# A two-layer decoder trunk on one core: 21 instead of 19 look-ahead groups, a new spacing of them, and the next chunk's weights split ahead of the second set of u dots

## The chip, the cores and the metric

The kernel runs on one core of one Trainium2 chip. The metric is the device time of one execution in microseconds (us). A profiled execution gives, beside its own time, a span (first to last instruction) and a trace of every engine: PE (matmuls), DVE (elementwise), ACT (activations, casts), POOL (here it issues gathers and scattered adds), SP (here it issues loads and stores).

## The reference

512 positions of width 1024 go through two layers. Each layer is a token mixer (layer 0: causal pooling beside retention; layer 1: a gated linear recurrence), an output projection, a residual and a layer norm, and then a PEER channel mixer with a residual and a layer norm. The change lies in PEER alone:

```python
q = (xt @ w_q).reshape(T, 8, 2, 128)
s = einsum('thpd,hpkd->thpk', q, sub_keys)
s_top, i_top = top_k(s, 16)
cand = s_top[:, :, 0, :, None] + s_top[:, :, 1, None, :]       # 256 per head
cand_id = i_top[:, :, 0, :, None] * 128 + i_top[:, :, 1, None, :]
best, pos = top_k(cand, 16)
eid = take_along_axis(cand_id, pos)                            # of 16384 experts
gate = softmax(best)
act = gelu(einsum('td,thkd->thk', xt, u_tab[eid]))
out = einsum('thk,thkd->td', gate * act, v_tab[eid])
```

## The kernel before

**How PEER is split.** The positions are four blocks of 128 (tb 0 to 3). Of 384 positions (tb 0 to 2) the sum over experts is made densely: 128 blocks of 128 experts, gathered into 32 groups of four. Per block, `mm1` (24 matmuls of 128x352, lines 185 to 187) makes x·u for 352 positions, ACT applies gelu into a tile `ge`, the result is multiplied with a dense gate tile `gt` (line 1059), and `mm2` (line 1096; 18 matmuls of 128x512: three position blocks, three products, two halves) multiplies with v. The last 128 positions, and the first 32 in another way, take gathered rows: `gather_rounds` fetches one u row and one v row per position and chosen expert (line 968), DVE makes a dot (line 980) and a weighted sum (line 993); for the 32 positions the u dots alone are gathered (`Scatter`, lines 102 to 105, gathers at line 741), and POOL adds their weights to a table `gz` (line 127).

**Hi and lo.** A product of float32 matrices is three passes: each weight block of 128x1024 is loaded by SP into one of five `raw` buffers, cast by ACT to `hi` (line 169), and DVE subtracts to make `lo` (line 170); the pairs have six buffers. Of each three matmuls, lines 185 and 186 use `hi` and line 187 uses `lo`.

**The stages of a layer.** Mixer and output projection; then `route_topk`, four chunks c of two heads each; then "choose" of tb 3, 1 and 2 (the second top-k, the softmax and `lookup`, all on DVE, and three transposes on PE, line 834); then `route_gates`, eight slices of two half-slices, each of which makes one-hot tiles `oh` and `og` on DVE (lines 900, 901), 32 small matmuls on PE (lines 910, 911), and a store of the slice's gates to `gd` in memory (line 916); then `experts`, which reads `gd` and `gz` back into `gt`. A chunk of `route_topk` begins with a projection of all 512 positions by four weight blocks w0 to w3 of `wq` (`proj_T`, 96 matmuls of 128x512, also on lines 185 to 187). If `self.w0` holds blocks that were split earlier, `wchunk` takes those; before the change, `route_topk` never sets it. Behind the projection follow, for each tb, the score matmuls and the top-k on DVE, and after tb 2 and tb 3 four u dots each.

**Work made ahead.** So that PE has work beside the routing, `lookahead` is a generator of `mm1` blocks: NLA groups of four. `peer` steps it by a credit: the two routing generators yield costs, and each 2.8 of credit takes one block. Blocks left when both generators have ended are made behind the last gate slice. The finished `ge` of a group is stored to memory (`sp`), except the last KEEP = 2 groups, and read back in `experts`. In `experts` such a group ("old") needs no `mm1` of its own and a "fresh" one does; fresh and old groups are interleaved, `mm1` runs four blocks ahead, and the gather rounds are paced with one unit per old block and two per fresh block.

**What sets the order.** The program text and the credit give the order in which work is handed to a list scheduler, which fixes the order of the instructions on each engine before the run. At run time each engine takes its instructions strictly in that order and waits, where it must, for buffers and semaphores.

Of the kernel before, what the change touches and what calls it, by code (L numbers as in the profile page):

```python
# [37 lines left out]
GQ = 8  # L38
LAG = GQ + 4
NSD = TD // 32  # L40
NLA = 19
NSZ = 4
KEEP = 2
ROT = 3
RAW = 5
QS = 8
Y2 = 1.85
YC = (1.5, 3.0, 3.0, 4.0)
AHEAD = 4
TAIL = 4  # L50
# [92 lines left out]
class Kern:  # L143
# [612 lines left out]
    def lookahead(self, layer, xT, sp):  # L756
        for g in range(NLA):
            ge = self.pe.tile([P, NB, TN], F32, name="ge", tag="ge", bufs=3)
# [8 lines left out]
    def route_topk(self, layer, xT, kT, gz):  # L767
        nc, tc, io = self.nc, self.tc, self.io
        with tc.tile_pool(name="rt", bufs=1) as rt, tc.tile_pool(name="rt2", bufs=2) as rt2, \
                tc.tile_pool(name="rs2", bufs=1) as rs2:  # L770
            i16 = rt.tile([P, 16], F16, name="i16", tag="i16")
            nc.gpsimd.iota(i16, pattern=[[1, 16]], base=0, channel_multiplier=0, allow_small_or_imprecise_dtypes=True)
            thr = rt.tile([P, 16], F16, name="thr", tag="thr")
            nc.sync.dma_start(out=thr, in_=io["thr"])
            stop = rt.tile([P, NTB, 16, 16], F32, name="stop", tag="stop")
            itop = rt.tile([P, NTB, 16, 16], F16, name="itop", tag="itop")
            wq = io["peer_w_q"][layer]

            def sink_q(n, ps):
                q = rt2.tile([P, T], F32, name="qh", tag="qh", bufs=5)  # L780
                nc.scalar.copy(q, ps)
                qs.append(q)

            def choose(tb, h0, n):
                sv = stop[:, tb, h0 * 2:(h0 + n) * 2].rearrange("p (h two) s -> p h two s", two=2)
                s0, s1 = sv[:, :, 0, :], sv[:, :, 1, :]
                iv = itop[:, tb, h0 * 2:(h0 + n) * 2].rearrange("p (h two) s -> p h two s", two=2)
                i0, i1 = iv[:, :, 0, :], iv[:, :, 1, :]
                cand = rs2.tile([P, 8, 64], F32, name="cand", tag="cand")
                at = 0  # L790
                for a, b, m in ((0, 1, 16), (1, 4, 8), (4, 8, 4), (8, 16, 1)):
                    w = b - a
                    ov = cand[:, :n, at:at + w * m].rearrange("p h (i j) -> p h i j", j=m)
                    nc.vector.tensor_tensor(ov, s0[:, :, a:b, None].broadcast_to([P, n, w, m]),
                                            s1[:, :, None, 0:m].broadcast_to([P, n, w, m]), ALU.add)
                    at += w * m
                best = rs2.tile([P, 8, 16], F32, name="best", tag="best")[:, :n]
                pos = rs2.tile([P, 8, 16], U32, name="pos", tag="pos")[:, :n]
                for h in range(n):
                    c2 = rs2.tile([P, 64], F32, name="c2", tag="c2")  # L800
                    cv = cand[:, h, :]
                    nc.vector.max(out=best[:, h, 0:8], in_=cv)
                    nc.vector.max_index(out=pos[:, h, 0:8], in_max=best[:, h, 0:8], in_values=cv)
                    nc.vector.match_replace(out=c2, in_to_replace=best[:, h, 0:8], in_values=cv, imm_value=NEG)
                    nc.vector.max(out=best[:, h, 8:16], in_=c2)
                    nc.vector.max_index(out=pos[:, h, 8:16], in_max=best[:, h, 8:16], in_values=c2)
                    yield 0.7
                if tb == 3:
                    gate = self.gate3.rearrange("p (h s) -> p h s", h=8)
                elif tb == 0:  # L810
                    gate = gz.gate[h0 // 2]
                else:
                    gate = rs2.tile([P, 8, 16], F32, name="gate", tag="gate")
                nc.vector.tensor_tensor(gate, best, best[:, :, 0:1].broadcast_to([P, n, 16]), ALU.subtract)
                nc.scalar.activation(gate, gate, AF.Exp)
                sm = rs2.tile([P, 8], F32, name="gsm", tag="gsm")[:, :n]
                nc.vector.tensor_reduce(sm, gate, AX.X, ALU.add)
                nc.vector.reciprocal(sm, sm)
                nc.vector.tensor_tensor(gate, gate, sm[:, :, None].broadcast_to([P, n, 16]), ALU.mult)
                kk = yield from self.lookup(rs2, pos, i0, i1, thr, i16)  # L820
                fl = "p h s -> p (h s)"
                if tb == 3:
                    nc.vector.scalar_tensor_tensor(self.eid, kk[0].rearrange(fl), 128.0, kk[1].rearrange(fl),
                                                   ALU.mult, ALU.add)
                    return
                if tb == 0:
                    gz.place(self, rs2, h0 // 2, kk[0].rearrange(fl), kk[1].rearrange(fl))
                    return
                tg = slice((tb - 1) * P // GW, tb * P // GW)
                ghT, glT = kT[:, tg, 2, :], kT[:, tg, 3, :]  # L830
                yield 2.8
                pt = self.psC.tile([P, 512], F32, name="pC", tag="pC")
                for i, t in enumerate((kk[0], kk[1], gate)):
                    nc.tensor.transpose(pt[:, i * P:(i + 1) * P], t.rearrange(fl), self.ident)
                px = pt[:, :3 * P].rearrange("p (i g w) -> p i g w", i=3, w=GW)
                nc.scalar.copy(kT[:, tg, 0:2, :].rearrange("p g i w -> p i g w"), px[:, 0:2])
                gs = rs2.tile([P, P // GW, GW], F32, name="gs", tag="gs")
                nc.scalar.mul(gs, px[:, 2], GS)
                nc.scalar.copy(ghT, gs)
                nc.vector.tensor_tensor(glT, gs, ghT, ALU.subtract)  # L840

            for c in range(4):
                qs = []
                keys = rt2.tile([P, 4, P], F32, name="keys", tag="keys")
                nc.sync.dma_start(out=keys, in_=io["keysT"][layer][:, c * 4:c * 4 + 4, :])
                self.proj_T(wq, c, xT, sink_q, early=c == 0)
                for tb in range(NTB):
                    ts = slice(tb * P, (tb + 1) * P)
                    ps = self.psB.tile([P, 512], F32, name="pB", tag="pB")
                    for i in range(4):  # L850
                        nc.tensor.matmul(ps[:, i * P:(i + 1) * P], qs[i][:, ts], keys[:, i, :],  # L851
                                         start=True, stop=True)
                    ixs = rs2.tile([P, 4, 16], U32, name="ix", tag="ix", bufs=2)
                    for i in range(4):
                        hp = c * 4 + i
                        sc = ps[:, i * P:(i + 1) * P]
                        mx = stop[:, tb, hp, :]
                        ix = ixs[:, i, :]
                        s2 = rs2.tile([P, P], F32, name="s2", tag="s2")
                        nc.vector.max(out=mx[:, 0:8], in_=sc)  # L860
                        nc.vector.max_index(out=ix[:, 0:8], in_max=mx[:, 0:8], in_values=sc)
                        nc.vector.match_replace(out=s2, in_to_replace=mx[:, 0:8], in_values=sc, imm_value=NEG)
                        nc.vector.max(out=mx[:, 8:16], in_=s2)
                        top = nc.vector.max_index(out=ix[:, 8:16], in_max=mx[:, 8:16], in_values=s2)
                    nc.vector.tensor_copy(itop[:, tb, c * 4:c * 4 + 4, :], ixs)
                    yield YC[c]
                    if tb == 0:
                        yield from choose(0, c * 2, 2)
                        if c:
                            gz.add(self)  # L870
                    else:
                        n = (0, 1, 1)[tb - 1] * QC // 2
                        yield 1.3 * n
                        with tc.issue_after(top.ins):
                            gz.dots(self, n)
                gz.weigh(self, rs2)
                if c == 0:
                    gz.add(self)
            gz.add(self, 8)
            for tb in (3, 1, 2):  # L880
                yield from choose(tb, 0, 8)
# [347 lines left out]
```

## Time and profile before

| | us |
|---|---|
| median of 3 runs | 2803.01 |
| lowest, highest | 2802.81, 2809.61 |
| profiled execution, its own time | 2803.68 |
| its span | 2801.9 |
| PE busy | 2745.8 (98%) |
| DVE busy | 2359.3 (84%) |

The profiled execution is 0.67 us above the median and 1.8 us above its span. Its mean granted PE clock is 0.992. Layer 0's PEER lies at about 200 to 1350 us of the span (choose about 440 to 505, gates to 613, experts from there), layer 1's at about 1660 to the end. In the wait views, a row is the waiting engine, tile and line, what it waited for, and then the total in us, the times and the longest. In the window views a row is the stretch, its length, then busy time and instruction count of PE, PEld (weight loads), DVE, ACT and POOL, the granted PE clock, the DMA engines' busy share, and GB/s. In timelines and chains a row begins with the start and the duration in us.

### The profile page before, as it was taken

How to read it: one execution, taken by the hardware profiler on the slowest of the kernel's cores; microseconds unless marked ns; L12 is line 12 of the kernel's file. 1: busy time of each engine (PE TensorE's matmuls, PEld its weight loads, DVE VectorE, ACT ScalarE, POOL GpSimd, SP SyncE). 2: the span in 40 equal slices, each digit the busy share in tenths (PEclk: the TensorE clock that was granted, in tenths of full speed). 3: DMA queues.
4: the chain of work that ended last, by engine and by line, in shares of the span. 5: the costliest groups of instructions: out<-in, count | busy, mean ns of one | idle time of the engine just before them, and what ended most of it. 6: DMA issues, size and time to landing. Idle time of an engine off the chain costs nothing.

```text
span 2801.9 us, 41670 instructions
## 1 busy us (share of the span) xinstructions
PE 2745.8 (98%) x15314; PEld 2449.4 (87%) x15314; DVE 2359.3 (84%) x4556; ACT 1116.5 (40%) x1575; POOL 1352.6 (48%) x865
## 2 busy tenths in 40 slices
PE   9999999999999999999999999999989999999998
PEld 7899899988888888888788898999978888888886
DVE  6678989867898989888798677899868888988887
ACT  3353336543333333333334343445543333333332
POOL 0006667864565666553000017667764556555651
PEclk9999999999999999999999999999999999999999
DMA  6357776999999999998222557686999999999993
GB/s 228 127 178 227 236 221 178 248 270 366 382 386 382 390 377 396 374 383 295 95 83 72 203 177 203 194 245 177 277 308 361 378 398 368 389 388 382 384 383 146
DMA packets 318318, 788.34 MB, mean 281 GB/s; under 512 B 62113, under 2 KB 128161, under 8 KB 318113
## 3 DMA queue, kind: packets, MB, share of 16 engines
q1 hardware_dynamic: 175808, 410.75, 41.4%
q0 software_dynamic: 120128, 303.22, 32.0%
q10 hardware_dynamic: 22176, 71.71, 6.4%
q8 instruction: 120, 1.97, 0.3%
q14 instruction: 86, 0.70, 0.1%
HBM read 708.50 MB, written 77.07 MB: 280 GB/s over the span
## 4 chain that ended last, share of the span: by engine, by line
PE 86%; DVE 7%; DMA 3%; POOL 2%; issue 1%; ACT 1%; SPq 0%; DVEq 0%; POOLq 0%; ACTq 0%
PE pB L1096 18%; PE pC L1096 18%; PE pA L187 12%; PE pA L185 12%; PE pA L186 12%; PE pC L185 2%; PE pC L186 2%; PE pC L187 2%; POOL gz L127 2%; DMA urow<-in_u,ids 2%; DVE lo L170 1%; PE pB L910 1%; DMA gd<-gbuf 1%; PE pB L911 1%; PE pB L851 1%
## 5 line engine op out<-in xcount | busy, mean ns | idle before, releaser
L169 ACT CAST hi<-raw 128x1024 fp32r<-128x1024 f32 (+1 forms) x609 | 637.8, 1050 | 962.9 <-PE pC L1096 368.2
L170 DVE TENSOR_TENSOR lo<-raw,hi 128x1024 fp32r<-128x1024 f32 (+1 forms) x609 | 733.7, 1215 | 184.5 <-ACT hi L169 156.4
L187 PE MATMUL pA<-xThi,lo 128*128 128x352 f32 (+2 forms) x1872 | 628.7, 336 | 11.2 <-DVE lo L170 11.2
L185 PE MATMUL pA<-xThi,hi 128*128 128x352 f32 (+2 forms) x1872 | 631.2, 337 | 0.6 <-ACT hi L169 0.3
L968 POOL DMA_INDIRECT row<-in_u,eid x256 | 407.3, 1591 | 464.4 <-DVE av L980 369.2
L186 PE MATMUL pA<-xTlo,hi 128*128 128x352 f32 (+2 forms) x1872 | 627.4, 335 | 0.6 <-DVE xTlo L170 0.6
L127 POOL DMA_INDIRECT gz<-gate,idx x256 | 486.2, 1899 | 130.6 <-issue 84.2
L968 POOL DMA_INDIRECT row<-in_v,eid x256 | 361.9, 1414 | 145.1 <-issue 58.5
L187 PEld LDWEIGHTS pA<-xThi,lo 128*128 128x128 f32 x1872 | 353.7, 189 | 28.6 <-DVE lo L170 14.1
L185 PEld LDWEIGHTS pA<-xThi,hi 128*128 128x128 f32 x1872 | 354.0, 189 | 18.3 <-ACT hi L169 1.2
L186 PEld LDWEIGHTS pA<-xTlo,hi 128*128 128x128 f32 x1872 | 353.9, 189 | 17.3 <-DVE xTlo L170 1.2
L993 DVE SCALAR_TENSOR_TENSOR h<-row,cf,h 128x1024 f32<-128x1024 f32 x256 | 329.4, 1287 | 6.7 <-DMA row<-in_v,eid 6.4
L980 DVE CUSTOM_DVE_ANT_0 row<-row,x 128x1024 f32<-128x1024 f32 x256 | 311.6, 1219 | 10.0 <-DMA row<-in_u,eid 9.7
L1096 PE MATMUL pB<-hi,ch 128*128 128x512 f32 x768 | 300.2, 391 | 17.9 <-DMA raw<-in_peer_ut 9.7
L1096 PE MATMUL pC<-hi,ch 128*128 128x512 f32 x768 | 299.9, 390 | 0.0
L1096 PE MATMUL pC<-lo,ch 128*128 128x512 f32 x768 | 299.6, 390 | 0.0
L1096 PE MATMUL pB<-hi,cl 128*128 128x512 f32 x768 | 299.6, 390 | 0.0
L1096 PE MATMUL pB<-lo,ch 128*128 128x512 f32 x768 | 299.5, 390 | 0.0
L1096 PE MATMUL pC<-hi,cl 128*128 128x512 f32 x768 | 299.3, 390 | 0.0
L170 DVE TENSOR_TENSOR cl<-gt,ch 128x768 fp32r<-128x768 f32 x128 | 122.0, 953 | 117.0 <-ACT ch L169 117.0
L741 POOL DMA_INDIRECT urow<-in_u,ids x64 | 86.9, 1358 | 273.4 <-ACT ids L87 203.7
L169 ACT CAST ch<-gt 128x768 fp32r<-128x768 f32 x128 | 107.2, 837 | 249.4 <-PE pC L1096 152.2
(280 smaller groups left out, 4541.9 us busy)
## 6 DMA issues: line engine op xcount, KB each, us to landing
raw<-in_peer_ut SPq DMA_DIRECT2D x256, 512.0 KB
raw<-in_peer_v SPq DMA_DIRECT2D x256, 512.0 KB
gd<-gbuf SPq DMA_DIRECT2D x16, 2048.0 KB
gt<-gd ACTq DMA_DIRECT2D x60, 512.0 KB
sp<-ge SPq DMA_DIRECT2D x34, 704.0 KB
ge<-sp ACTq DMA_DIRECT2D x34, 704.0 KB
raw<-in_peer_w_q SPq DMA_DIRECT2D x32, 512.0 KB
gz<-zero SPq DMA_DIRECT2D x64, 256.0 KB
```

The costliest lines, as they stand in the source:

```text
L127: d = nc.gpsimd.indirect_dma_start(out=flat, out_offset=bass.IndirectOffsetOnAxis(ap=self.idx[c][:, j:j + 1], axis=0), in_=gate[:, j:j + 1 ...
L169: self.nc.scalar.copy(hi, src)
L170: return self.nc.vector.tensor_tensor(lo, src, hi.bitcast(F32), ALU.subtract)
L185: nc.tensor.matmul(ps, ah, bh, start=(first and i == 0), stop=False)
L186: nc.tensor.matmul(ps, ah, bl, start=False, stop=False)
L187: nc.tensor.matmul(ps, al, bh, start=False, stop=(last and i == n - 1))
L741: d = self.nc.gpsimd.indirect_dma_start(out=t, out_offset=None, in_=self.io["u%d" % layer], in_offset=bass.IndirectOffsetOnAxis(ap=ids[:, ...
L851: nc.tensor.matmul(ps[:, i * P:(i + 1) * P], qs[i][:, ts], keys[:, i, :], start=True, stop=True)
L968: nc.gpsimd.indirect_dma_start(out=t, out_offset=None, in_=io[name], in_offset=bass.IndirectOffsetOnAxis(ap=at, axis=0))
L980: dot = nc.vector.tensor_tensor_reduce(ur, ur, x, 1.0, 0.0, ALU.mult, ALU.add, av[:, k:k + 1])
L993: nc.vector.scalar_tensor_tensor(acc, vr, c, acc, ALU.mult, ALU.add)
L1096: nc.tensor.matmul(acc[hf], a[:, ts], b[:, hf * 512:(hf + 1) * 512], start=first and i == 0, stop=last and i == 2)
```

## The change

- `NLA` goes from 19 to 21: 84 blocks made ahead in each layer instead of 76; 44 instead of 52 are made fresh in `experts`.
- `Y2`, half the cost that each gate slice's half yields, goes from 1.85 to 1.6, so that the gates draw fewer blocks.
- In choose, the cost yielded per head goes from 0.7 to 1.2 for tb 1, 2 and 3.
- In `route_topk`, for chunks 0 to 2, the four weight blocks of the next chunk's projection are loaded and split (`self.w0`) in the program ahead of the yield and the u dots behind tb 3, instead of at the head of the next chunk.

```diff
-NLA = 19
+NLA = 21
...
-Y2 = 1.85
+Y2 = 1.6
...
-                    yield 0.7
+                    yield 0.7 if tb == 0 else 1.2
...
                         n = (0, 1, 1)[tb - 1] * QC // 2
+                        if tb == 3 and c < 3:
+                            self.w0 = [self.stream(wq[c + 1, k]) for k in range(4)]
                         yield 1.3 * n
                         with tc.issue_after(top.ins):
                             gz.dots(self, n)
```

Lines behind the inserted two have numbers higher by two in the changed kernel (1059 becomes 1061, 901 becomes 903).

What the order of the instructions shows, the same in both layers: in choose, 19 blocks of `mm1` stand ahead of the first transposes (line 834) instead of 16, and 9 instead of 7 between the first and the last of them; inside the gate slices stand 373 matmuls of `mm1` instead of 444, now one block per half-slice, and 16 splits instead of 19; behind the last gate matmul and ahead of the first `mm2` stand 216 matmuls of `mm1` (nine blocks) instead of 73.

Three places in layer 0. PE at the third chunk's start (pC_2818 and pC_2842 are look-ahead blocks, pA_2881 is the projection's first output), before:

```order
L185 MATMUL pC_2818<-xThi_88,hi_2814 128x352
...
L187 MATMUL pC_2818<-xThi_88,lo_2815 128x352
L185 MATMUL pA_2881<-xThi_88,hi_2859 128x512
...
L187 MATMUL pA_2881<-xThi_88,lo_2872 128x512
```

and now:

```order
L185 MATMUL pC_2842<-xThi_88,hi_2838 128x352
L186 MATMUL pC_2842<-xTlo_89,hi_2838 128x352
L185 MATMUL pA_2881<-xThi_88,hi_2814 128x512
...
L187 MATMUL pA_2881<-xThi_88,lo_2827 128x512
L185 MATMUL pA_2881<-xThi_88,hi_2826 128x512
L187 MATMUL pC_2842<-xThi_88,lo_2839 128x352
```

Before, three whole look-ahead blocks (72 matmuls) stood ahead of the projection, whose 15th matmul was the first to read lo_2872. Now two whole blocks and two matmuls of a third stand there, then 16 matmuls of the projection, and then the third block's first use of its own lo_2839.

DVE at the same place, before (the rows on line 105 are the second set of dots; rows of the top-k are left out):

```order
L170 TENSOR_TENSOR lo_2866<-raw_2863,hi_2865 128x1024
...
L105 ISA urow_2482,avu_2498<-urow_2482,xx_1402 128x1024
...
L170 TENSOR_TENSOR lo_2872<-raw_2869,hi_2871 128x1024
...
L170 TENSOR_TENSOR lo_2878<-raw_2875,hi_2877 128x1024
```

and now:

```order
L170 TENSOR_TENSOR lo_2827<-raw_2824,hi_2826 128x1024
...
L105 ISA urow_2482,avu_2498<-urow_2482,xx_1402 128x1024
...
L170 TENSOR_TENSOR lo_2833<-raw_2830,hi_2832 128x1024
...
L170 TENSOR_TENSOR lo_2839<-raw_2836,hi_2838 128x1024
```

The places of the three splits are the same rows of DVE's order. Before, they made lo of w1, w2 and w3 of the chunk; now they make lo of w2, w3 and the look-ahead block. One weight moved ahead of the dots, and a look-ahead block went behind them.

DVE behind the last gate slice, before (lo_6972 and on are splits for line 185 to 187 and for v, ch and cl the split of gate times gelu):

```order
L901 TENSOR_TENSOR og_6717<-oh_6716,kT_1455 128x2048
L170 TENSOR_TENSOR lo_6972<-raw_6969,hi_6971 128x1024
...
L170 TENSOR_TENSOR lo_7044<-raw_7041,hi_7043 128x1024
L1059 TENSOR_TENSOR gt_6761<-gt_6761,ge_6760 128x11x64
```

and now:

```order
L903 TENSOR_TENSOR og_6816<-oh_6815,kT_1455 128x2048
L170 TENSOR_TENSOR lo_7030<-raw_7027,hi_7029 128x1024
...
L170 TENSOR_TENSOR lo_7241<-raw_7238,hi_7240 128x1024
L1061 TENSOR_TENSOR gt_7021<-gt_7021,ge_7020 128x11x64
```

Between the last one-hot tile and the first gate multiply stand eight splits instead of four; the last four are of v blocks.

## Prediction

> **What bounds the kernel now.** I read the engines' busy times first, then what PE waited for, then those waits stretch by stretch, and last the windows and timelines at the places that the change touches.
>
> ```profile
> PE 2745.8 (98%) x15314; PEld 2449.4 (87%) x15314; DVE 2359.3 (84%) x4556; ACT 1116.5 (40%) x1575; POOL 1352.6 (48%) x865
> PE pA L187 <- DVE lo L170: 11.2, 7, 3.3
> PE pB L1096 <- DMA raw<-in_peer_ut: 9.7, 1, 9.7
> PE pB L1096 <- ACT ch L169: 8.2, 2, 7.4
> PE pC L834 <- DVE ka L954: 3.4, 1, 3.4
> PE pC L834 <- issue: 3.3, 1, 3.3
> ```
>
> PE is busy for all but 56 us of the span, and the change removes no arithmetic from it: the same blocks are made, in other places. So it can gain only where PE idles, or runs at a reduced clock after idling, and it loses where it opens a new wait. The second and third rows are one place, once in each layer: the first `mm2`, where PE has run out of work while the gates are still on their way through memory. The last two are choose, one per layer. The first is mostly the chunks' starts, where a matmul waits for a split.
>
> In stretches around the start of the second chunk (212:232), of the third (268:294 and, in layer 1, 1715:1740) and around choose (445:485, 1895:1930), PE's waits read, in this order:
>
> ```profile
> PE pA L187 <- DVE lo L170: 1.7, 1, 1.7
> PE pA L187 <- DVE lo L170: 3.3, 2, 2.6
> PE pA L187 <- DVE lo L170: 3.3, 1, 3.3
> PE pC L834 <- DVE kb L954: 0.7, 1, 0.7
> PE pA L187 <- DVE lo L170: 1.1, 1, 1.1
> PE pA L187 <- DVE lo L170: 0.6, 1, 0.6
> ```
>
> The kb row of 0.7 is in both choose windows, the 1.1 is layer 0's and the 0.6 layer 1's. What such waits cost beyond themselves shows in the granted clock:
>
> ```profile
> 285.00:290.00 5.00, 1.80 (x7) 1.20 (x8) 5.00 (x23) 0.00 (x0) 4.37 (x3) 1.00 0.91 313
> 470.00:475.00 5.00, 3.60 (x13) 3.44 (x14) 5.00 (x29) 0.85 (x3) 4.08 (x4) 0.60 0.37 15
> 475.00:480.00 5.00, 5.00 (x25) 5.00 (x24) 5.00 (x16) 1.36 (x2) 4.39 (x3) 0.72 0.83 221
> 630.00:635.00 5.00, 3.12 (x8) 2.51 (x9) 3.08 (x4) 0.83 (x1) 3.04 (x2) 0.52 1.03 416
> 1735.00:1740.00 5.00, 5.00 (x12) 3.96 (x13) 5.00 (x20) 0.38 (x1) 4.39 (x3) 0.50 1.02 323
> 1920.00:1925.00 5.00, 4.33 (x18) 4.14 (x19) 5.00 (x27) 0.85 (x3) 4.09 (x4) 0.66 0.48 84
> 2080.00:2085.00 5.00, 3.71 (x9) 2.94 (x10) 2.48 (x4) 0.83 (x1) 2.12 (x3) 0.50 1.02 418
> ```
>
> The 2.6 us wait near 285 left the clock at 1.00; those of 3.3 us and more were followed by 0.50 to 0.72. Busy time times the missing share is what the clock cost: 3.60 x 0.40 + 5.00 x 0.28 = 2.8 us in layer 0's choose, 4.33 x 0.34 = 1.5 in layer 1's, 3.12 x 0.48 = 1.5 and 3.71 x 0.50 = 1.9 behind the gates, 2.5 at the third chunk of layer 1.
>
> **The durations.** Starts of matmuls in PE's timeline, and a run of `mm2` in the chain; the last row is from the list of DMA issues:
>
> ```profile
> 599.89 0.32 PE L187 MATMUL pA<-xThi,lo 128*128 128x352 f32 x1
> 600.36 0.32 PE L187 MATMUL pA<-xThi,lo 128*128 128x352 f32 x1
> 604.93 0.22 PE L910 MATMUL pB<-og,oh 128*128 128x128 f16 x1
> 605.50 0.22 PE L910 MATMUL pB<-og,oh 128*128 128x128 f16 x1
> 1323.89 2.75 PE pB L1096 x12
> sp<-ge SPq DMA_DIRECT2D x34, 704.0 KB
> ```
>
> Three apart, 0.47 us: 0.158 per `mm1` matmul, 3.79 per block of 24. Ten apart, 0.57: 0.057 per gate matmul. 2.75 / 12 = 0.229 per 512-wide matmul, which I use for the projections too.
>
> **The tail behind the gates: gain 9.7 + 11.6.** In layer 0, the last gate store and the first gate multiply are
>
> ```profile
> 613.58 9.28 DMA gd<-gbuf
> 630.07 0.89 DVE L1059 TENSOR_TENSOR gt<-gt,ge 128x704 f32<-128x704 f32 x1 [3.44 <-DMA gt<-gz]
> ```
>
> so from the last store to the end of the cast that frees PE (0.9 behind the multiply) it is 613.6 to 631.9, 18 us, and the gate matmuls end a little before the store. Before, 73 x 0.158 = 11.5 us of matmuls stood there; now 216 x 0.158 = 34.1. The idle time of 8.2 (layer 0) and 9.7 (layer 1) is covered with about 15 us to spare. What is late next is DVE's own order: the multiply now stands behind eight splits, the last of which takes a buffer that about the seventh block of nine frees, at 26.5 us; split 1.2, multiply 0.9 and cast 0.9 (ACT has little else) make 29.5, still 4.6 ahead of PE. SP's loads of v and gates are no later than that: they are queued behind one v load at most. With the clock, 8.2 + 1.5 and 9.7 + 1.9.
>
> **Choose: gain 7.4 + 5.7.** Five blocks more stand beside it: 5 x 3.79 = 19 us of PE work, for 5 x 1.2 = 6 us of splits on DVE, which is at 5.00 of 5.00 in the windows above and sets the pace. The 13 us net are more than what PE loses there now: 3.3 + 0.7 + 1.1 and 2.8 of clock in layer 0, 3.4 + 0.7 + 0.6 and 1.5 in layer 1. I leave 0.5 in each for small waits that stay: 7.9 - 0.5 and 6.2 - 0.5. The two extra stores of `ge` (704 KB each) fall where 15 to 221 GB/s are moved, at no cost; without that cover they would be the 2 us or so that 0.7 MB takes at 418 GB/s.
>
> **Gates: loss 2.6 in each layer.** PE loses 71 matmuls there, DVE only three splits. DVE's half-slice:
>
> ```profile
> 517.04 2.35 DVE L900 TENSOR_TENSOR oh<-iot,kT 128x2048 f16<-128x2048 f16 x2
> 519.31 2.36 DVE L901 TENSOR_TENSOR og<-oh,kT 128x2048 f16<-128x2048 f16 x2
> 521.62 1.23 DVE L170 TENSOR_TENSOR lo<-raw,hi 128x1024 fp32r<-128x1024 f32 x1
> 522.76 2.36 DVE L900 TENSOR_TENSOR oh<-iot,kT 128x2048 f16<-128x2048 f16 x2
> ```
>
> From one to the next 5.7 us, by durations 5.9: 16 of them are 91 to 95. PE needs 373 x 0.158 + 512 x 0.057 = 88.1 to 88.6. So DVE becomes the bound by 2.6 to 6.4 us. I take the lower end, because starts are 5.7 apart; 0 is the other end, if DVE enters the gates ahead of PE.
>
> **The chunk starts: loss 6.6 + 5.3 at the third chunk, 0.8 at the fourth, 0.4 at the second.** The hoist brings forward twelve SP loads per layer, their ACT casts and DVE splits; each takes the place in its queue of a look-ahead block's load, cast or split, which goes back. At the third chunk the two sets have only changed places around the dots. DVE and the gathers' chain in layer 0, and DVE in layer 1:
>
> ```profile
> 271.50 8.64 DMA urow<-in_u,ids
> 280.17 1.23 DVE L105 CUSTOM_DVE_ANT_0 urow<-urow,xx 128x1024 f32<-128x1024 f32 x1 [6.88 <-DMA urow<-in_u,ids]
> 286.27 1.20 DVE L170 TENSOR_TENSOR lo<-raw,hi 128x1024 fp32r<-128x1024 f32 x1
> 288.59 1.21 DVE L170 TENSOR_TENSOR lo<-raw,hi 128x1024 fp32r<-128x1024 f32 x1
> 1733.69 1.21 DVE L170 TENSOR_TENSOR lo<-raw,hi 128x1024 fp32r<-128x1024 f32 x1
> 1736.01 1.21 DVE L170 TENSOR_TENSOR lo<-raw,hi 128x1024 fp32r<-128x1024 f32 x1
> ```
>
> The gathered rows land at 280.1 whatever PE does, and DVE, in its order, holds the splits behind the dots. Before, PE did 72 x 0.158 + 14 x 0.229 = 14.6 us of work until it wanted the split that ends at 287.5; it waited 2.6 for it, so it came at 284.9. Now it does 50 x 0.158 + 16 x 0.229 = 11.6 and wants the one that ends at 289.8: it comes at 281.9 and waits 7.9, where it waited 3.3 in all. That is 4.6 more, and by the rows above a wait as long as that costs about 2 of clock (0 to 2.8): 6.6. In layer 1 it came at 1734.9 - 3.3 = 1731.6; now 3.0 earlier, waiting until 1737.2, which is 8.6 instead of 3.3; the clock is at 0.50 there already, so 5.3.
>
> The Trainium skill (TensorE: Matmul & The Clock Gate, Part 1) states that a window of about 3.4 us of idleness halves the clock and about as long a busy one restores it. The rows agree that 2.6 us leaves it whole and 7 us halves it; at 1735 it stayed at 0.50 for all of 5 us, so one window is too few, and by the page the clock's 2 would be an estimated 1.7.
>
> At the second chunk two blocks' matmuls now stand in the projection, and the order leaves a stall of about 2.1 where 1.7 was, 0.4 (layer 1: 0.5). At the fourth, the split that PE needs has moved behind one more, with no wait there before: 0.8, half of the 0 to 2 that one split's distance (2.3 between starts) can cost.
>
> **Experts: loss 1 in each layer.** Eight blocks' `mm1` leave this stage, 8 x 3.79 = 30.3 us; they are back as five in choose, minus three in the gates, six behind them.
>
> ```profile
> 650.00:1300.00 650.00, 650.00 (x3213) 569.17 (x3212) 572.12 (x657) 235.19 (x284) 366.50 (x242) 1.00 0.98 380
> 655.00:660.00 5.00, 5.00 (x24) 4.13 (x22) 4.45 (x7) 2.22 (x3) 2.62 (x2) 1.00 1.02 416
> POOL row L968 <- DVE av L980: 192.1, 50, 10.5
> ```
>
> Now the stage is 52 x (3.79 + 18 x 0.229) + 76 x 18 x 0.229 = 725 us by PE, and will be 694. DVE is at 88%; with eight splits less (9.8 us) it has 628 of 694, 90.5%. The bytes shrink by 8 x 0.52 and grow by two groups read back, 1.44: 275 MB become 273, so 380 GB/s become 393. No PE wait is in this stage now; runs of old blocks, denser in bytes, get longer, which may cost 0 to 8 us. I take 1, near to what it shows now.
>
> **Sum.** Layer 0: 9.7 + 7.4 - 2.6 - 6.6 - 0.8 - 0.4 - 1 = 5.7. Layer 1: 11.6 + 5.7 - 2.6 - 5.3 - 0.8 - 0.5 - 1 = 7.1. Together 12.8: the span goes from 2801.9 to 2789.1, and the profiled time, 1.8 above its span, from 2803.68 to 2790.9. The median before is 0.67 lower than the profiled time, so a median of about 2790; with the terms' coarseness I say 2791. Its own range: clock 0 to 2.8, gates 0 to 6.4, fourth chunk 0 to 2 and experts 0 to 8 in each layer do not all fall on one side; 2780 to 2800.
>
> About 0.3% (8.4 us) is what a measurement of this kernel tells from no change: faster is below 2794.6, slower above 2811.4.
>
> **Rivals.**
>
> *Experts bound by DMA: slower.* If 380 GB/s, with the engines' share at 0.98, is already all that this mix of gathers and blocks gets, the stage shrinks only by its bytes, 2.7 MB or 7 us, and not by 30; 23 us of waiting for rows or blocks come back in each layer. 2791 + 46 - 2 = 2835. Against it: windows of 416 and more, no PE wait in 650 us, and POOL held back for 192 us by DVE, not by a transfer. It decides from a ceiling below 393; a ceiling of 388 would cost 9 us a layer and end near 2808. The Trainium skill (DMA: Bandwidth & Descriptors, Specifications) gives about 358 GB/s as a core's share of memory, by which the rival would hold; the measured 380 is over it. Chance 0.1.
>
> *DVE takes the place of the stalls: no change.* The gates cost 6.4 each instead of 2.6 (7.6 more) and the experts 3 each instead of 1 (4 more), since DVE, at 90% there, has longer runs of old blocks: 2791 + 11.6 = 2803. For it: DVE at 5.00 in the choose windows and back to back in the gates. Chance 0.2.
>
> *The hoist does what it says: faster.* If the rows of u land earlier than in this trace, or the order left the splits ahead of the dots, the third chunk waits for nothing: 11.9 come back and the 6.6 of waits that it has now go, 2791 - 18.5 = 2772. Against it is the fixed order: a look-ahead block's split stands behind the dots, and PE wants it sooner. Chance 0.06.
>
> My forecast keeps 0.64: 0.54 of it below 2794.6 and 0.1 above. Faster: 0.54 + 0.06 = 0.6. Slower: 0.08 of the first rival's 0.1. Same: 0.1 + 0.2 + 0.02 = 0.32. The range reaches from 2778, part of the way to the third, to 2804, which takes in the second; about 0.2 is outside.
>
> **What would show it.** Right: no PE wait at the first `mm2` in either layer, none over 1 us on the transposes, and a single wait of about 8 us per layer for a split at the third chunk's start, with the clock near 0.5 behind it; small waits on gates for `oh` or `og`; none in the experts at about 393 GB/s. Wrong: PE waiting for v or rows in the experts, the first `mm2` still waiting, or no long wait at the third chunk.

## The result and the profile after

The changed kernel takes 2781.89 us (median of 4 runs, 2778.31 to 2782.76) against 2802.91 for the kernel before in the same comparison; the ratio is 0.9917, interval 0.9900 to 0.9935. That is 21.0 us less, where 12 were forecast (2791). The profiled execution is the fastest of the four, 2778.31, 25.4 under the profiled execution of before, and 3.6 under its own median; the last section shows a difference of that size between traces. In experiments 7 and 11 one run each was slow (3393 and 3892 us, at a granted clock of 0.75 and 0.65), and the times given there are medians of the other ten.

The first row of the changed kernel's page, and then the first of PE's waits in it (waiting tile and line, what it waited for, total us, times, longest):

```profile
PE 2737.3 (99%) x15314; PEld 2442.9 (88%) x15314; DVE 2357.4 (85%) x4556; ACT 1115.1 (40%) x1575; POOL 1342.4 (48%) x865
```

```profile
PE pC L187 <- DVE lo L170: 15.4, 6, 7.0
PE pC L252 <- DVE h L288: 2.1, 1, 2.1
PE pA L187 <- DVE lo L170: 1.9, 3, 0.9
PE pA L185 <- ACT hi L169: 1.4, 2, 0.7
PE pC L1108 <- POOL z L1105: 1.3, 1, 1.3
PE pB L1098 <- DVE cl L170: 1.1, 1, 1.1
```

The two rows on the first `mm2` (9.7 and 8.2 us) and the rows on the transposes of choose are gone. One row leads in their place: a look-ahead block's matmul, in a pC tile, that waits for its own split. Its two long cases are the third chunk's starts, 6.9 us in layer 0 and 7.0 in layer 1. PE is idle for 39 us instead of 56, and busy for 8.5 us less with the same 15314 matmuls, mostly since it runs less often at a reduced clock: its mean granted clock is 0.995 instead of 0.992.

Here are windows at the third chunk's start in the changed kernel, and DVE's timeline at the same place (the four u dots, the weight's split, the look-ahead block's split):

```profile
285.00:290.00 5.00, 0.00 (x0) 0.00 (x0) 5.00 (x20) 0.00 (x0) 3.80 (x4) 0.65 0.84 258
290.00:295.00 5.00, 4.83 (x21) 4.83 (x22) 4.93 (x19) 0.00 (x0) 4.39 (x3) 0.66 0.99 289
```

```profile
277.06 1.23 DVE L105 CUSTOM_DVE_ANT_0 urow<-urow,xx 128x1024 f32<-128x1024 f32 x1 [2.42 <-DMA urow<-in_u,ids]
...
284.23 1.24 DVE L105 CUSTOM_DVE_ANT_0 urow<-urow,xx 128x1024 f32<-128x1024 f32 x1 [0.29 <-DMA urow<-in_u,ids]
286.60 1.20 DVE L170 TENSOR_TENSOR lo<-raw,hi 128x1024 fp32r<-128x1024 f32 x1
288.91 1.20 DVE L170 TENSOR_TENSOR lo<-raw,hi 128x1024 fp32r<-128x1024 f32 x1
```

PE stands still through the whole of 285 to 290 while DVE is busy through it; the second split ends at 290.1, and PE goes on at a clock of 0.66. In layer 1 the wait ends at 1726.1, and the windows behind it are

```profile
1725.00:1730.00 5.00, 3.86 (x13) 3.86 (x14) 4.93 (x16) 0.00 (x0) 4.54 (x2) 0.50 0.91 285
1730.00:1735.00 5.00, 5.00 (x26) 4.45 (x25) 5.00 (x10) 2.68 (x7) 4.25 (x3) 0.96 0.78 225
```

To see where the time went I cut each layer at matmuls that both kernels have. First and last starts of the last one-hot matmuls and of the first `mm2` come from the views by line; the kernel before in the first fence, the changed one in the second, layer 0 ahead of layer 1:

```profile
L910 PE MATMUL pC<-og,oh x64: 218/218/218, 510.5 to 612.6; 128*128 128x128 f16 x64
L1096 PE MATMUL pB<-hi,ch x384: 389/389/796, 631.9 to 1336.7; 128*128 128x512 f32 x192
...
L910 PE MATMUL pC<-og,oh x64: 218/218/218, 1957.3 to 2059.7; 128*128 128x128 f16 x64
L1096 PE MATMUL pB<-hi,ch x384: 389/389/795, 2081.3 to 2785.5; 128*128 128x512 f32 x192
```

```profile
L912 PE MATMUL pC<-og,oh x64: 218/219/219, 526.4 to 618.1; 128*128 128x128 f16 x64
L1098 PE MATMUL pB<-hi,ch x384: 388/389/501, 652.5 to 1325.8; 128*128 128x512 f32 x192
...
L912 PE MATMUL pC<-og,oh x64: 217/218/219, 1962.8 to 2054.2; 128*128 128x128 f16 x64
L1098 PE MATMUL pB<-hi,ch x384: 388/390/396, 2088.6 to 2760.1; 128*128 128x512 f32 x192
```

Between the last one-hot matmul and the first `mm2` lie 19.3 and 21.6 us before, 34.4 after: 73 matmuls of 0.158 and a wait before, 216 (34.1 us) and no wait after. Done so for every stage, with the matmuls that stand in it by the order subtracted (0.158 each for `mm1`, 0.227 for the 512-wide, 0.057 for the gates', 0.06 for scores and transposes), the time above the matmuls is, in us:

| stage | layer 0 before | after | layer 1 before | after | gain, both | forecast |
|---|---|---|---|---|---|---|
| to the second chunk's scores | 5.3 | 6.7 | 5.0 | 6.6 | -3.0 | -0.9 |
| to the third chunk's | 6.9 | 12.1 | 9.7 | 12.3 | -7.8 | -11.9 |
| to the fourth chunk's | 3.1 | 3.7 | 3.1 | 3.8 | -1.3 | -1.6 |
| choose, to the first gate matmul | 13.6 | 3.8 | 11.3 | 3.8 | +17.3 | +13.1 |
| gates | 4.4 | 5.3 | 4.7 | 5.0 | -1.2 | -5.2 |
| behind the gates | 7.7 | 0.2 | 10.0 | 0.2 | +17.3 | +21.3 |
| experts | 4.6 | 3.5 | 3.3 | 0.9 | +3.5 | -2.0 |

The gains come to 24.8, and the spans differ by 25.4; 0.2 of the rest lies outside these stages, and 0.4 is rounding. Where PE doesn't wait, as in choose after, what is left is the coarseness of the spacings, so the table is to be read for its differences.

### The profile page after: what moved, and what is told of

The parts are those of the page before. It is cut to its first block, busy times and chain, and to the rows that moved or that the text cites. A ratio compares the mean times of both kernels' runs of the same rounds, so it can differ in the third digit from the quotient of the medians.

```text
span 2776.5 us, 41653 instructions
## 1 busy us (share of the span) xinstructions
PE 2737.3 (99%) x15314; PEld 2442.9 (88%) x15314; DVE 2357.4 (85%) x4556; ACT 1115.1 (40%) x1575; POOL 1342.4 (48%) x865
## 4 chain that ended last, share of the span: by engine, by line
PE 83%; DVE 6%; DMA 4%; issue 4%; POOL 3%; ACT 0%; SPq 0%; DVEq 0%; POOLq 0%; ACTq 0%
PE pC L1098 15%; PE pB L1098 15%; PE pA L187 12%; PE pA L185 12%; PE pA L186 12%; PE pC L187 3%; PE pC L185 3%; PE pC L186 3%; DMA row<-in_v,eid 2%; POOL row L970 1%; DMA urow<-in_u,ids 1%; DVE lo L170 1%; POOL gz L127 1%; PE pB L912 1%; PE pB L913 1%
## 5 line engine op out<-in xcount | busy, mean ns | idle before, releaser
L185 PE MATMUL pA<-xThi,hi 128*128 128x352 f32 (+2 forms) x1808 | 607.5, 336 | 1.9 <-ACT hi L169 1.4
L187 PE MATMUL pA<-xThi,lo 128*128 128x352 f32 (+2 forms) x1808 | 605.0, 335 | 1.9 <-DVE lo L170 1.9
L186 PE MATMUL pA<-xTlo,hi 128*128 128x352 f32 (+2 forms) x1808 | 604.8, 334 | 0.6 <-DVE xTlo L170 0.6
L185 PEld LDWEIGHTS pA<-xThi,hi 128*128 128x128 f32 x1808 | 340.1, 188 | 19.0 <-ACT hi L169 2.5
L187 PEld LDWEIGHTS pA<-xThi,lo 128*128 128x128 f32 x1808 | 340.0, 188 | 17.4 <-DVE lo L170 3.1
L186 PEld LDWEIGHTS pA<-xTlo,hi 128*128 128x128 f32 x1808 | 340.1, 188 | 16.7 <-DVE xTlo L170 1.2
L187 PE MATMUL pC<-xThi,lo 128*128 128x352 f32 x672 | 218.6, 325 | 15.4 <-DVE lo L170 15.4
```

Of the source, the lines that this page charges most:

```text
L185: nc.tensor.matmul(ps, ah, bh, start=(first and i == 0), stop=False)
L186: nc.tensor.matmul(ps, ah, bl, start=False, stop=False)
L187: nc.tensor.matmul(ps, al, bh, start=False, stop=(last and i == n - 1))
```

## The experiments

**1. Without the hoist.**

```diff
-                        if tb == 3 and c < 3:
-                            self.w0 = [self.stream(wq[c + 1, k]) for k in range(4)]
```

> The changed kernel without the hoisted splits; 21 groups, the gates' 1.6 and choose's 1.2 stay. Theory: the hoist only cost time. From the traces of before and after, the three chunk starts took 7.2 us more in layer 0 and 4.9 more in layer 1 for the same matmuls, so without it 2782 - 12 = 2770, with the long split wait at the third chunk at 2.6 instead of 6.9. Rival: the hoist helps as its description says (the next chunk's weights are ready), and the long wait belongs to the denser look-ahead: then it is slower than 2782, by 5 or more, and the 6.9 stays.

Measured: 2768.26 us, ratio to before 0.9878 (0.9863 to 0.9893), 13.6 less than the changed kernel. PE's waits lead with

```profile
PE pA L187 <- DVE lo L170: 10.5, 5, 4.1
```

and at the third chunk's start of layer 0 they are 3.8 in all. The stages to the second, third and fourth chunk are at 5.4, 7.8, 3.1 and 4.2, 10.2, 3.1; the others are as in the changed kernel to within 1 us, but for layer 0's experts, which lose 1.8 less. The hoist only costs.

**2. The hoist alone.** The kernel before, with the two lines of the hoist and nothing else of the change.

> The kernel before with the hoisted splits alone; 19 groups, 1.85 and 0.7 as before. Theory: slower by the 12 us that the chunk starts took more, 2815, with the waits at the first expert matmul and in choose as before. Rival: 2803 or faster, if the hoist gives back in choose or later what it costs at the starts.

Measured: 2816.47, ratio 1.0047 (1.0034 to 1.0061), 13.9 over before. The waits of before are all there, and the hoist's beside them:

```profile
PE pC L187 <- DVE lo L170: 17.1, 6, 8.5
PE pB L1098 <- ACT ch L169: 15.9, 2, 9.0
...
PE pC L834 <- DVE ka L956: 3.4, 1, 3.4
PE pC L834 <- issue: 3.3, 1, 3.3
```

So the two parts add: +13.9 alone, and without it -34.3, make -20.4, where both together measured -21.0.

**3. Four more blocks, all behind the gates.**

```diff
-NLA = 19
+NLA = 20
```

> The kernel before with 20 groups instead of 19 and nothing else, so that the four more blocks all fall behind the last gate slice (168 matmuls there instead of 73). Theory: only the wait at the first expert matmul goes, 7.5 us in layer 0 and 9.8 in layer 1, and the waits in choose stay: 2803 - 17 = 2786. Rival: what is removed there comes back, since four blocks and a group read back make the expert stage denser in bytes: no more than 8 us gained.

Measured: 2783.39, ratio 0.9928 (0.9915 to 0.9942): 19.2 less than before, from this one number. No wait on the first `mm2` is left among PE's waits; those of choose are as they were:

```profile
PE pC L834 <- DVE ka L954: 3.4, 1, 3.4
PE pC L834 <- issue: 3.3, 1, 3.3
```

The remaining 15 us of experiment 1's gain are what this one lacks: choose, with one more group. In the traces its choose stages lose 16 us more than those of experiment 1. No run changes choose alone, so choose's price is known from this difference.

**4. Three blocks moved back into the gates.**

```diff
-Y2 = 1.6
+Y2 = 1.95
```

> The changed kernel with the gates' yield at 1.95 instead of 1.6: the gates take three blocks more (445 matmuls, as before the change), and 144 matmuls are left behind them instead of 216. Theory: 144 x 0.158 = 22.8 us still cover the 18 to 21 us that the gates need through memory, so 2782 to 2785 with at most 2 us of wait per layer at the first expert matmul; the four blocks left over are more than is needed. Rival: the cover must be as long as the splits that stand ahead of the gate multiply on DVE, and waits of 5 us or more per layer come back: 2792 or more.

Measured: 2784.02, ratio 0.9930 (0.9916 to 0.9943), whose interval overlaps the changed kernel's. The first `mm2` itself waits for nothing; about 10 us behind it PE waits for a cast, 2.2 us in layer 0 and 1.2 in layer 1:

```profile
PE pB L1098 <- ACT ch L169: 3.5, 2, 2.2
```

So some 23 us of matmuls behind the gates do nearly all; 34 are a reserve.

**5. The hoist at the third chunk alone.**

```diff
-                        if tb == 3 and c < 3:
+                        if tb == 3 and c == 1:
```

> The changed kernel with the hoist at the third chunk's start alone (for chunk 1 only; chunks 0 and 2 as before). Theory: of the hoist's 12 us, this start has the 5.2 and 2.6 that the traces of before and after differ by between the first score matmuls of the second and the third chunk: 2768 + 8 = 2776, with the 7 us waits for the look-ahead block's split. Rival: each of the three starts costs alike, since the hoist costs by its loads and splits and not by its place: 2772.

Measured: 2779.51, ratio 0.9917 (0.9903 to 0.9931), 11 over experiment 1. Two waits at the third chunk's starts make it, 7.6 in layer 0 and 9.0 in layer 1:

```profile
PE pC L187 <- DVE lo L170: 16.6, 2, 9.0
```

The stage to the third chunk is at 13.4 and 13.7 instead of 7.8 and 10.2, 9 of the 11 us. So four hoisted splits at this one place cost most of what twelve cost in all (11 of 13.6). The prices of the three places don't add: in the changed kernel, with all twelve, this stage is only 6.4 above experiment 1. There the rows land earlier: layer 0's first dot starts at 277.1, here at 279.9, and the split that PE waits for ends about 1 us earlier.

**6. Later adds, without the hoist.** In the kernel before, sixteen scattered adds stood on POOL ahead of the second chunk's gathers; here they are made one chunk later.

```diff
-                if c == 0:
-                    gz.add(self)
             gz.add(self, 8)
```

> The changed kernel without the hoist, and without the first head's sixteen scattered adds at the end of chunk 0 (they are made one chunk later, the rest at the end as before). Theory: those adds stand on POOL ahead of chunk 1's gathers of u rows, the rows land late, DVE waits for them in its order, and the weights' splits stand behind the dots; without them the third chunk's start costs what the fourth's does. Between first score matmuls it took 7.8 and 10.2 us over the sum of its matmuls in the run without the hoist, the fourth start 3.1: 2768 - 4.7 - 7.1 = 2756, and no wait for a split over 1 us there. Rival: the sixteen adds, 32 us of POOL, come back behind the gates, where the experts wait for the table: 2768 or more with a wait at the first expert matmul.

Measured: 2790.96, ratio 0.9957 (0.9943 to 0.9971). Both halves of the expectation came true at once: the stage to the third chunk fell to 3.4 and 3.0, as the fourth's, with no wait there; and the rival's price was higher than that gain. PE's waits and the row of ACT's timeline behind the gates:

```profile
PE pA L185 <- ACT ge L754: 32.0, 3, 16.8
```

```profile
643.84 1.04 ACT L169 CAST hi<-raw 128x1024 fp32r<-128x1024 f32 x1 [23.25 <-DMA gz<-gate,idx]
```

The last add is issued at 640.2 instead of 613.3 in experiment 1. ACT issues the read of the table for the experts' third group, and the read waits for the adds; for 23 us ACT casts nothing, and PE runs out of split blocks. The wait is not where the rival had put it, at the first expert matmul, but ahead of it.

**7. Later adds, with the hoist.** The edit of experiment 6 in the changed kernel.

> The same later adds with the hoist, as in the changed kernel. Theory: the hoist costs at the third start only because DVE is held at the dots by late rows while the look-ahead block's split stands behind them; with the rows early it costs only what it does at the other two starts, some 4 us over both layers: 4 above the run of the later adds without the hoist, about 2760. Rival: the hoist's price is the order alone, whenever rows land: 12 above it, about 2768.

Measured: 2801.60, ratio 0.9993 (0.9983 to 1.0003), 10.6 over experiment 6: near the rival's 12, and not the 4. The waits at the third chunk's starts, in layer 0 and then in layer 1, are

```profile
PE pC L187 <- DVE lo L170: 4.0, 1, 4.0
PE pC L187 <- DVE lo L170: 2.9, 1, 2.9
```

in place of 6.9 and 7.0. So rows that land late are 2.9 us of the wait in layer 0 and 4.1 in layer 1, about half of it. The hoist's price at this place did not fall by that: the stage to the third chunk is 5.5 and 4.8 worse than in experiment 6, 10.3 together, against 6.4 between the changed kernel and experiment 1, since without the hoist early rows leave no wait here at all. In layer 0 the last two dots wait 1.3 and 1.5 us for their rows, in experiment 6 2.4 and 1.2, and there PE doesn't wait; so with rows that land about alike, what differs is the order, which puts the look-ahead block's split behind the dots while PE has less work ahead of it.

**8. Thin gates, without the hoist.**

```diff
-Y2 = 1.6
+Y2 = 0.5
```

> The changed kernel without the hoist and with the gates' yield at 0.5 instead of 1.6: 205 matmuls of mm1 in the gate slices instead of 373, 384 behind them instead of 216. Theory: PE would need 66 us for the slices (matmuls plus the 4.4 us that they took over their sum in all traces so far), DVE by starts 16 x 4.54 and some nine splits of 1.13, 82; so here DVE is the bound, and 16 us per layer are lost: 2768 + 32 = 2800. Rival: DVE's work on the gates is not near a bound at any load, 2768.

Measured: 2816.66, ratio 1.0046 (1.0032 to 1.0060), 48 over experiment 1. DVE is the bound here:

```profile
PE pB L910 <- DVE og L901: 30.2, 19, 3.8
```

The slices took 87.6 and 88.9 us, 5 to 7 more than expected. By the order ten splits stand among DVE's gate work there, so 16 x 4.54 + 10 x 1.13 = 84 would be DVE's own need; the rest are waits of DVE itself, 4.3 us in layer 0 and 5.8 in layer 1, mostly for casts and buffers of those splits. PE's loss over its matmuls grew by 22 and 23 us in the two layers, 45 of the 48. A lighter PE doesn't make the stage shorter than about 88.

**9. 22 groups, without the hoist.**

```diff
-NLA = 21
+NLA = 22
```

> The changed kernel without the hoist, with 22 groups instead of 21: four more blocks behind the gates (312 matmuls there instead of 216), four fewer in the experts. Theory: 21 groups already cover the way of the gates through memory, so nothing is left for more of them to remove: 2768, within 4. Rival: the expert stage runs at its limit in bytes, and its next four blocks less leave waits there: 2775 or more.

Measured: 2774.98, ratio 0.9900 (0.9885 to 0.9915), 6.7 over experiment 1: more than the theory's 4, less than the rival's 7 by little. The experts show a trace of what the rival says,

```profile
PE pB L1096 <- ACT ch L169: 2.0, 3, 1.1
```

and their two stages lost 4.0 us together. The gates lost 1, and 3.5 lie in choose, between the transposes: that is the slower spacing told of at the end. Experiment 12, also with 22 groups, has it in layer 0 alone, so I don't put it down to the 22nd group. 21 groups are enough; a 22nd costs some 3 to 4.

**10 and 11. Later adds with 22 and with 23 groups.** Experiment 6 with `NLA = 22` and `NLA = 23`.

> The later adds (no hoist) with 22 groups. In the run of the later adds with 21 groups the third chunk's start lost its waits as expected, but ACT stood for 23 us behind a read of the table in its queue, since the adds ended 32 us later, and PE waited 16.8 and 15.2 us for it. Theory: four more blocks, 15 us, stand ahead of that read: only about 1.6 us of the wait are left in a layer, 2768 - 11.6 + 3 = 2760. Rival: the read moves forward with the blocks, and the wait stays: 2785 or more.

> The later adds (no hoist) with 23 groups. Theory: 30 us more of matmuls stand behind the gates, the wait is gone altogether, 2757, unless the denser expert stage waits. Rival: with 36 fresh blocks the experts' bytes bind: PE waits in that stage and 2768 or more.

Measured: 2793.16, ratio 0.9956 (0.9942 to 0.9970), and 2793.48, ratio 0.9966 (0.9955 to 0.9976). PE's waits, first of 22 and then of 23 groups:

```profile
PE pA L185 <- ACT ge L754: 22.0, 3, 12.3
```

```profile
PE pB L1094 <- ACT ch L169: 11.0, 6, 3.9
PE pA L185 <- ACT ge L754: 4.6, 2, 2.8
PE pB L1094 <- DVE cl L170: 4.2, 5, 1.1
```

Theory missed in both. With 22 the wait behind the gates fell by 10 of 32 us and not by 29: the read stays early in ACT's order, and ACT stood at it for 22.8 us where it had stood for 23.3. With 23 it is nearly gone, but the experts' stage, with 36 fresh blocks, now waits by itself, 15 us in eleven pieces. Ahead of the longest of them (3.9 us) ACT had itself waited 5.9 us for the load of a v block, and the windows of 100 us with the longer waits move 391 to 406 GB/s. That is what the expert rival of the prediction looks like, four groups beyond the kernel before; that the bytes are what binds isn't shown, since experiment 1 moves 407 without a wait.

**12. Later adds with 22 groups, the table read on POOL.**

```diff
-                gz.read(q if n > 1 else nc.gpsimd, gt[:, :NSZ], g)
+                gz.read(q if n > 3 else nc.gpsimd, gt[:, :NSZ], g)
```

> As the later adds with 22 groups, and the reads of the scattered table for the third and fourth group of the experts are issued by POOL, behind the adds, instead of by ACT. In the run without this, PE waited 12.3 and 9.7 us for gelu on ACT behind the gates. Theory: that wait is ACT's queue standing at a read that the adds hold up; with the read on POOL, ACT casts on, the wait goes and 22 us with it: 2793 - 22 = 2771, of which some 7 us are what 22 groups cost over 21. Rival: the table itself is late, the first gate multiply waits for it, and PE waits as long for its cast: 2788 or more.

Measured: 2770.55, ratio 0.9879 (0.9862 to 0.9895), 22.6 less than with 22 groups alone. The wait for gelu on ACT is gone from PE's waits, whose largest row is now

```profile
PE pA L187 <- DVE lo L170: 4.2, 3, 2.7
```

It was ACT's queue. With this, the rows land early, the third chunk starts without a wait (3.3 and 3.4), and the adds' delay costs 2.7 us behind the gates, in layer 0 alone. The time is that of experiment 1, no better: what is gained at the third chunk goes to the 22nd group, to the denser experts and to that rest.

## Why the prediction was right

Its sign held, and so did its mechanism at every place but the gates and the experts, whose losses hardly came. Its size held less well: 12 us were forecast and 21 came, so that the median lies at the lower end of the range of 2780 to 2800. By the table, choose, the third chunk, the gates and the experts each came out 4 to 6 us better than forecast, and the stage behind the gates and the second chunk 4 and 2 us worse; that these errors partly cancel is luck.

**Behind the gates.** Forecast +21.3, shown 17.3 in this stage and, alone (experiment 3), 19.2. The 18 us way of the gates through memory and the split's place in DVE's order were read rightly. The cast that frees PE ended 3.6 us ahead of need; 4.6 were forecast. Part of the gain that was counted here (a clock of 0.50 to 0.52 behind the wait) lies in the experts' stage in the table, since that stage begins with the first `mm2`. Experiment 3, which changes the tail alone, shows it there too: its experts' stages lose 3.5 less than before. Of the 8.2 us that the forecast took for layer 0's first `mm2`, 0.8 was a second wait, 10 us later.

**Choose.** Forecast +13.1, shown 17.3. All waits and all loss of clock went, as worked out. Of the excess of 4.2, 1.0 is the small waits that the forecast left in, and about 1.3 is the slower spacing of the matmuls in layer 0 of the kernel before, told of below, which nothing ties to the change. The rest stays open.

**The third chunk.** Forecast -11.9, shown -7.8. Which split PE waits for, and that it waits for one long time, was right. The failing steps are "it comes at 281.9 and waits 7.9", where it waited 6.9, with "8.6 instead of 3.3", where it was 7.0. PE came later than the sums said, since the second chunk's starts had lost 1.4 and 1.6 us more and not the 0.4 and 0.5 of the forecast, while layer 0's splits ended at 290.1 and not much later than the 289.8 of before. What PE loses at the second chunk it doesn't wait at the third, as long as the splits end when they did. With a clock of 0.66 behind it (4.83 x 0.34 = 1.6 us) that makes 6.9 - 3.3 + 1.6 = 5.2, the table's number. In layer 1 the wait is 3.7 longer than before. The forecast let the clock cost there what it did; by windows of 5 us it cost 2.1 (3.86 x 0.50 + 5.00 x 0.04) instead of 2.9 (5.00 x 0.50 + 5.00 x 0.07), and 0.3 of other loss went, which makes the table's 2.6. Taking out the hoist gave 13.6 (experiment 1), adding it cost 13.9 (experiment 2), against the 14.4 that the forecast has for the three starts.

The Trainium skill's rule of one window of about 3.4 us (TensorE: Matmul & The Clock Gate, Part 1) came nearer here than the rows of before: the 1.6 us of lost clock in layer 0 agree with its estimated 1.7. In layer 1 the same product gives 2.1.

**The second chunk.** Forecast -0.9, shown -3.0 against the trace of before. That stage varies by itself: 4.2 to 7.4 in the executions without the hoist at this place, 5.5 to 7.1 in those with it. How much of the 3.0 the hoist makes stays open.

**Gates.** Forecast -5.2, shown -1.2. The failing step is "PE needs 373 x 0.158 + 512 x 0.057 = 88.1 to 88.6. So DVE becomes the bound". PE took 4.4 and 4.7 us more than the sum of its matmuls for these slices before the change, which the forecast's own trace would have shown; so its need was 92.5, and DVE with 16 half-slices of 5.7, 91, was just below it. What the 4.4 consist of no run here shows. The small waits for `oh` or `og` that were to be the sign of it didn't come: in the changed kernel PE waits for nothing in the gates. In the changed kernel's timeline DVE still makes a half-slice in 5.68:

```profile
526.88 2.36 DVE L902 TENSOR_TENSOR oh<-iot,kT 128x2048 f16<-128x2048 f16 x2
532.56 2.36 DVE L902 TENSOR_TENSOR oh<-iot,kT 128x2048 f16<-128x2048 f16 x2
```

Without the hoist the stage took 92.5 in both layers. That DVE is near was right: experiment 8 shows that the stage doesn't go below about 88.

**Experts.** Forecast -2, shown +3.5, of which the tail's clock is 3.4 by the forecast's own products; with it taken out, about 0. The rival of a DMA ceiling fell: in the changed kernel the stage waits once, for 1.1 us, and moves 389 GB/s from 660 to 1300, where 393 were forecast. The trace of experiment 1 has whole 100 us stretches above its 393 GB/s without a wait on PE:

```profile
800.00:900.00 100.00, 100.00 (x500) 87.95 (x500) 93.00 (x108) 37.28 (x45) 61.42 (x40) 1.00 1.02 407
```

By the Trainium skill (DMA: Bandwidth & Descriptors, Specifications) about 358 GB/s would be the share of a core; 407 over 100 us shows that it doesn't bind in these runs.

**The hoist does what it says.** This rival fell in experiments 1 and 2, by the reason given against it, the fixed order; in experiment 7 layer 0's first dot starts at 274.5 instead of 277.1, and waits of 4.0 and 2.9 us stay. The rival that DVE takes the place of the stalls fell too, since the gates lost 1.2 us and the experts nothing.

## What to carry to other kernels

When a change moves work and removes none, cut the trace at instructions that both kernels have, subtract the work of each stretch, and compare what is left; a stage's own overhead belongs in its need before another engine is called the bound. A prefetch that is fixed in an engine's order takes the place of something else: ask what was pushed back behind the next long wait, and who wants it first. A transfer that an engine with other work issues can hold that engine for as long as the transfer must wait, here ACT for 23 us.

## What the hardware showed unasked

In choose, between the transposes, `mm1` runs at one spacing in some traces and at another in others, and sometimes in the two layers of one trace, with no wait and no lower granted clock. These are windows of experiment 9's and then of experiment 1's kernel, at the same place of the same work:

```profile
495.00:500.00 5.00, 5.00 (x32) 5.00 (x31) 4.97 (x7) 4.99 (x8) 2.51 (x2) 1.00 0.62 118
500.00:505.00 5.00, 5.00 (x32) 5.00 (x31) 4.00 (x6) 2.11 (x5) 4.09 (x4) 1.00 0.91 247
```

```profile
495.00:500.00 5.00, 5.00 (x34) 5.00 (x33) 4.93 (x8) 5.00 (x9) 2.53 (x2) 1.00 0.72 157
500.00:505.00 5.00, 5.00 (x34) 5.00 (x33) 3.55 (x4) 2.61 (x4) 4.39 (x3) 1.00 0.98 288
```

PE is at 5.00 of 5.00 and at a clock of 1.00 in all four, but starts 32 matmuls or 34: 0.167 us apart or 0.158. The stage between the transposes takes 36.5 us or 34.7 by it, in each layer for itself. The kernel before has the slower spacing there in layer 0 (32 matmuls in each 5 us from 485 to 500), the changed kernel's profiled execution in neither layer; two such stages would make 3.6 us, as much as that execution lies under its median. Each kernel has one trace, so whether its other runs had the slower spacing isn't shown, and what sets it no run here shows.
